# A decoder block on one Trainium2 core: additions and a gate leave GpSimd for VectorE, and weights are split 1024 elements at a time

## Chip, cores and metric

The kernel runs on one core of one Trainium2 chip. The metric is the device time of one execution in microseconds (us), and a kernel's time is the median over its runs. The engines are named as in the profile: PE (TensorE; PEld is its weight load), DVE (VectorE), ACT (ScalarE), POOL (GpSimd) and SP (SyncE, which only issues DMAs here).

## What is computed

One decoder layer on x of 256 tokens by 1024 columns, all in float32:

```
mod = silu(c) @ w_ada + b_ada                       # 1024 x 6144
shift1, scale1, gate1, shift2, scale2, gate2 = split(mod, 6)
h = rms_norm(x, g_norm_mix) * (1 + scale1) + shift1
z = h @ w_in                                        # four mixers' inputs, then 4 x 1024 merge logits
y_n = mixer_n(z), n = 0..3                          # attention, gated linear attention, retention, window attention
mixed = sum_n sigmoid(merge_logits_n) * (y_n @ w_branch[n])
x = x + gate1 * (mixed @ w_out)
h2 = rms_norm(x, g_norm_ffn) * (1 + scale2) + shift2
x = x + gate2 * moe(h2)                             # 32 experts, the top 4 of each token, clamped SwiGLU
return rms_norm(x, g_final)
```

The change touches only what comes before the experts, called the front here: the six modulation vectors, the projections by `w_in`, `w_branch` and `w_out`, and the first residual sum.

## The kernel before

**Precision.** The front's products are made from three fp32r matmuls each: an operand is split into a high part (a copy rounded to fp32r) and a low part (the rest), and high by high, low by high and high by low are added up in PSUM. `split` (L308) does it for a weight tile: ACT writes the high part (L320), DVE subtracts it from the source (L321). The two parts live in pool `wp` with `WP` = 4 buffers of 512 columns each, so splits run ahead of the matmuls by a few pieces at most. Every engine works through its own instructions in order, so an instruction that waits holds up all that is queued behind it on that engine.

**Blocks.** For each of four blocks of 256 rows of `w_in`, `h_block` (L358) makes the block's scale and shift from columns of `w_ada` by matmuls, then the normed input's high part `hh` and low part `hl` (L376, every second one on POOL). The first 1024 columns of z (four tiles `c`) are summed up over these blocks.

**Units.** The other columns of z come in units of 256 columns (`z_unit`, L337): four splits of 128x512 (two rows of K by 256 columns), each followed by twelve matmuls of 128x256 (L334). After each split one step of a mixer (`bg()`) and one step of a modulation sum (`slow_step()`) are put into the program. The mixers are generators, so their instructions stand between those of the units.

**Modulation sums.** gate1, shift2, scale2 and gate2 are summed off the matmul engine by `ada` (L209), 512 columns at a time (`s_` is the vector, `j` the half): rows k = 0..3 are scaled on ACT (L223; for gate1 on POOL, L221) and added on POOL (L225), rows 4..7 are multiplied and added on DVE (L228) into `acs`. `ada_end` (L233) sums over the partitions by four PE transposes, a DVE reduction (L241) and a small addition (L242).

**Merge.** Sixteen units follow, four for each mixer branch in the order 0, 3, 1, 2 (`bi` counts them; unit 4 * `bi` + `u`). Each does a `z_unit`, a sigmoid on ACT (`msg`, L773), two splits of 128x256 of `w_branch` (`wl_b`, L774), twelve matmuls `pu` (L781), and on DVE `pu` * `msg` (L788). The sum over the branches, `mix`, is added on POOL (L789), on DVE for the last branch. At units 1, 3, ... 11 a modulation sum is ended and the next begun. In the last branch `mix` is split, and rows of `w_out` are loaded, multiplied by gate1 on POOL in 128x512 pieces (L746), split (`wl_o`) and multiplied with `mix` into `pw` (L737). `out_last` (L825) adds `pw` to `x_sb` on DVE (L830); the second norm and the router follow.

**Loads.** All weights go through a ring of 1 MB tiles, in the program's order on SP's queue: nine slots, from the third branch on sixteen. A load waits until the tile that its slot held has been read for the last time. The experts' weights follow in the same ring. Two late small loads, `b_down` and `g_final`, are issued by POOL (L926, L929).

## Time and profile before

| | |
|---|---|
| median of 3 runs | 1285.72 us (1283.94 to 1287.75) |
| span of the profiled execution (first to last instruction) | 1282.5 us |
| PE / DVE / ACT / POOL busy in it | 1208.7 / 484.3 / 204.4 / 134.3 us |
| moved | 469.90 MB, mean 366 GB/s |
| front / experts and last norm | first 321 us / the other 961 us |

The profiled execution's own time is not listed apart from its span; the span leaves out what lies before the first and after the last instruction, and it stands 3.2 us under the median of the runs. Busy time is summed over a window; a PE matmul's busy figure includes its pipeline, so two matmuls in a row overlap, and the distance between their starts is what one costs. "Idle before" is the time for which the engine did nothing ahead of the row, with the event that ended it.

### The profile page before, as it was taken

The page shows a single profiled execution, that of the slowest core. Times are in us where ns is not written, and L with a number is a line of the kernel's source. Part 1 is how long each engine was busy: PE and PEld are TensorE (multiplying, and loading weights), DVE is VectorE, ACT ScalarE, POOL GpSimd, SP SyncE. Part 2 cuts the span into 40 slices and gives each one's busy share as a digit, 9 for nine tenths or more (in the row PEclk, how much of TensorE's full clock was granted, in tenths as well). Part 3 has the DMA queues.
Part 4 walks back from the last instruction along what each step waited for, and adds up shares of the span by engine and source line. Part 5 has one row for each costly group of instructions (what it writes and reads, how often), then busy time and mean ns, then how long its engine had stood idle before and what let it go on. Part 6 is the DMA issues. An engine that isn't in the chain of part 4 may idle for free.

```text
span 1282.5 us, 15260 instructions
## 1 busy us (share of the span) xinstructions
PE 1208.7 (94%) x6202; PEld 568.3 (44%) x6202; DVE 484.3 (38%) x829; ACT 204.4 (16%) x403; POOL 134.3 (10%) x173
## 2 busy tenths in 40 slices
...
GB/s 337 333 191 259 117 239 393 372 102 290 291 371 398 421 414 420 413 419 417 417 418 416 419 414 421 413 421 413 422 413 421 414 420 415 418 417 415 419 380 154
DMA packets 117653, 469.90 MB, mean 366 GB/s; under 512 B 9933, under 2 KB 30506, under 8 KB 84810
## 3 DMA queue, kind: packets, MB, share of 16 engines
...
q0 software_dynamic: 192, 0.66, 0.2%
q10 hardware_dynamic: 408, 0.56, 0.1%
...
HBM read 467.80 MB, written 1.05 MB: 366 GB/s over the span
## 4 chain that ended last, share of the span: by engine, by line
PE 65%; DMA 19%; DVE 11%; issue 2%; ACT 1%; POOL 1%; ACTq 0%; POOLq 0%; SPq 0%; DVEq 0%
PE ea L1036 16%; PE eb L1036 14%; DMA wg<-in_w_gate_up_dram 12%; PE ed L1062 11%; DMA wd<-in_w_down_dram 5%; PE pz_m L334 4%; PE py L1072 4%; PE pg L971 2%; PE pw L737 2%; PE eb L1029 2%; PE pdl L1096 1%; PE ea L1029 1%; PE eat L1049 1%; PE pu L781 1%; DMA win_m<-in_w_in_dram 1%
## 5 line engine op out<-in xcount | busy, mean ns | idle before, releaser
L1036 PE MATMUL ea<-wg,he 128*64 128x512 f32 x1024 | 343.1, 600 | 7.0 <-DMA wg<-in_w_gate_up_dram 7.0
L1036 PE MATMUL eb<-wg,he 128*64 128x512 f32 x1024 | 336.9, 594 | 0.0
L1062 PE MATMUL ed<-wd,aT 128*64 128x512 f32 x960 | 216.1, 599 | 9.6 <-DMA wd<-in_w_down_dram 8.5
L1036 PEld LDWEIGHTS ea<-wg,he 128*64 128x64 f32 x1024 | 88.6, 136 | 168.3 <-issue 137.5
L1012 DVE TENSOR_SCALAR eg<-ea 128x512 f32<-128x512 f32 x32 | 22.1, 691 | 370.3 <-PE ea L1036 366.3
L1036 PEld LDWEIGHTS eb<-wg,he 128*64 128x64 f32 x1024 | 96.0, 137 | 146.8 <-issue 146.2
L1014 ACT ACTIVATE es<-eg 128x512 f32<-128x512 f32 x32 | 20.1, 630 | 844.1 <-DVE eg L1012 844.1
L1062 PEld LDWEIGHTS ed<-wd,aT 128*64 128x64 f32 x960 | 66.2, 137 | 146.9 <-issue 120.1
L995 POOL TENSOR_TENSOR pc<-pm,comb 128x128 f32<-128x128 f32 x64 | 23.5, 403 | 694.0 <-PE psm L1003 634.5
L334 PE MATMUL pz_m<-hh,wl_m 128*128 128x256 f32 x256 | 73.0, 285 | 3.1 <-DVE wl_m L321 3.0
L334 PE MATMUL pz_m<-hh,wh_m 128*128 128x256 f32 x256 | 73.4, 287 | 0.0
L334 PE MATMUL pz_m<-hl,wh_m 128*128 128x256 f32 x256 | 71.9, 281 | 0.0
L321 DVE TENSOR_TENSOR wl_m<-win_m,wh_m 128x512 fp32r<-128x512 f32 x64 | 53.5, 844 | 10.9 <-ACT wh_m L320 10.7
L1074 DVE TENSOR_TENSOR x_sb<-x_sb,py 128x512 f32<-128x512 f32 x60 | 41.2, 687 | 30.7 <-PE py L1072 30.7
L334 PEld LDWEIGHTS pz_m<-hh,wl_m 128*128 128x128 f32 x256 | 48.7, 190 | 5.1 <-DVE wl_m L321 4.9
L1029 PE MATMUL eb<-bgu,ident 32*64 32x512 f32 x128 | 49.2, 612 | 0.0
L334 PEld LDWEIGHTS pz_m<-hl,wh_m 128*128 128x128 f32 x256 | 49.0, 191 | 0.1
L334 PEld LDWEIGHTS pz_m<-hh,wh_m 128*128 128x128 f32 x256 | 48.7, 190 | 0.3
L320 ACT ACTIVATE wh_m<-win_m 128x512 fp32r<-128x512 f32 x64 | 38.8, 628 | 51.7 <-PE pz_m L334 18.5
L1065 DVE TENSOR_TENSOR oa<-ed,late 64x512 f32<-64x512 f32 x15 | 10.2, 683 | 96.0 <-PE ed L1062 96.0
L1065 DVE TENSOR_TENSOR ob<-ed,late 64x512 f32<-64x512 f32 x15 | 10.2, 683 | 91.2 <-PE ed L1062 91.2
L225 POOL TENSOR_TENSOR wada<-wada 128x512 f32<-128x512 f32 x24 | 36.8, 1532 | 61.6 <-ACT wada L223 60.8
...
## 6 DMA issues: line engine op xcount, KB each, us to landing
wg<-in_w_gate_up_dram SPq DMA_DIRECT2D x256, 1024.0 KB, 19.4
wd<-in_w_down_dram SPq DMA_DIRECT2D x120, 1024.0 KB, 19.1
...
win_c<-in_w_in_dram SPq DMA_DIRECT2D x10, 1024.0 KB, 11.8
...
```

The lines of the kernel that those rows point to most:

```text
L225: G.tensor_tensor(w[0], w[0], w[k], ALU.add)
L320: A.activation(wk, sk, AF.Copy)
L321: V.tensor_tensor(lk, sk, f32(wk), ALU.subtract)
L334: T.matmul(pz[:, b * 256:(b + 1) * 256], l, r, start=(kh == 0 and b == 0 and kk == 0 and i == 0), stop=last and i == 2, skip_group_check=True)
L737: T.matmul(pw[t, hf_], m_[:, kk, t * P:(t + 1) * P], w[:, 0, :], start=(k == 0 and i == 0), stop=(k == KC - 1 and i == 2))
L971: last_i["pg"] = T.matmul(pg[:, kk * 256:(kk + 1) * 256], n2[:, t, k * P:(k + 1) * P], pm[:, t].rearrange("p e s -> p (e s)"), start=(i == 0),
L995: G.tensor_tensor(pc[:, t, :, var, i ^ var, :], pv_[:, :, i, :], cv[:, :, i].unsqueeze(2).to_broadcast([P, EB // 2, CAP]), ALU.mult)
L1029: T.matmul(pp_[64 * j:64 * j + 64, :], ident[r:r + NE, r + e:r + e + 1].to_broadcast([NE, CAP]), bgu[r:r + NE, :], start=True, stop=False, ...
L1036: T.matmul(pp_[64 * j:64 * j + 64, :], he[:, k, (e % EB) * CAP:(e % EB + 1) * CAP], w[:, i * DE + j * 512:i * DE + (j + 1) * 512], start=F ...
L1062: T.matmul(pd[64 * jj:64 * jj + 64, :], aT[:, k % 4, 64 * (k // 4):64 * (k // 4) + 64], w[k % 2][:, o * 512:(o + 1) * 512], start=(k == 0) ...
L1072: T.matmul(py, s_[:, hf_, t * P:(t + 1) * P], o, start=True, stop=True)
L1074: V.tensor_tensor(yv, yv, py, ALU.add)
```

## The change

1. `split` makes pieces of up to 1024 elements per partition: the tiles of `wp` are twice as wide, with `WP` = 3 buffers. A unit has two splits of 128x1024 in place of four of 128x512, `w_branch` one of 128x512 in place of two of 128x256, `w_out` one of 128x1024 per row tile in place of two of 128x512.
2. `ada(s_, i)` loads 512 rows by 1024 columns (`i` is now the half of the rows) and sums all eight row tiles on DVE, 128x1024 at a time: one TENSOR_SCALAR and seven SCALAR_TENSOR_TENSOR per vector. ACT and POOL have no part in it. A step of `ada` is one row tile, so a call has four steps where it had eight.
3. `hl` and the `mix` addition are always on DVE.
4. `w_out` is no longer multiplied by gate1. `out_last` multiplies `pw` by gate1 (`gx`) and then adds it to `x_sb`, both on DVE.
5. `w_branch` comes as one tile, and the two late small loads are issued by ACT.

```diff
-WP = 4
+WP = 3
...
-    def ada(s_, j):
+    def ada(s_, i):
+        w = load_rows(f"wada{s_}_{i}", w_ada[0, i * 512:(i + 1) * 512, s_ * D:(s_ + 1) * D], D)
...
-            for k in range(4):
-                if s_ == 2:
-                    G.tensor_tensor(w[k], w[k], cact[:, k:k + 1].to_broadcast([P, 512]), ALU.mult)
+            for kk in range(4):
+                k = 4 * i + kk
+                if k == 0:
+                    V.tensor_scalar(acc, w[kk], cact[:, k:k + 1], None, ALU.mult)
                 else:
-                    A.activation(w[k], w[k], AF.Copy, scale=cact[:, k:k + 1])
-                if k:
-                    G.tensor_tensor(w[0], w[0], w[k], ALU.add)
+                    V.scalar_tensor_tensor(acc, w[kk], cact[:, k:k + 1], acc, ALU.mult, ALU.add)
                 yield
-            for k in range(4, KC):
-                V.scalar_tensor_tensor(acc, w[k], cact[:, k:k + 1], w[0] if k == 4 else acc, ALU.mult, ALU.add)
-                yield
...
     def ada_end(s_, i):
...
+        if i == 0:
+            return
...
-        for kh in range(4):
-            wh, wl = split(tiles[kh // 2][:, 2 * (kh % 2):2 * (kh % 2) + 2, c0:c0 + 256], 2, 256, f"{name}_{kh}", sw)
-            z_part(pz, wh, wl, kh, token)
-            bg()
-            slow_step()
+        for i in range(2):
+            wh, wl = split(tiles[i][:, :, c0:c0 + 256], 4, 256, f"{name}_{i}", sw)
+            for j in range(2):
+                z_part(pz, wh[:, 2 * j:2 * j + 2, :], wl[:, 2 * j:2 * j + 2, :], 2 * i + j, token)
+                bg()
+                slow_step()
...
-            (G if kk else V).tensor_tensor(hl[:, k, :], hf, f32(hh[:, k, :]), ALU.subtract)
+            V.tensor_tensor(hl[:, k, :], hf, f32(hh[:, k, :]), ALU.subtract)
...
-            for w in (wo[k], wo[k + 1]):
-                for h in range(2):
-                    c = slice(h * 512, (h + 1) * 512)
-                    G.tensor_tensor(w[:, c], w[:, c], gate1[:, c], ALU.mult)
-        cs = slice(hf_ * 512, (hf_ + 1) * 512)
-        held[k, hf_] = split(wo[k][:, cs].unsqueeze(1), 1, 512, f"o{k}{hf_}")
+        if hf_ == 0:
+            wh, wl = split(wo[k].rearrange("p (h f) -> p h f", h=2), 2, 512, f"o{k}")
+            for h in range(2):
+                held[k, h] = wh[:, h:h + 1, :], wl[:, h:h + 1, :]
...
-            wsp = [split(wb[k][:, u * 256:(u + 1) * 256].unsqueeze(1), 1, 256, f"b{n}_{u}{k}") for k in range(2)]
+            wbh, wbl = split(wb[:, :, u * 256:(u + 1) * 256], 2, 256, f"b{n}_{u}")
...
-                (V if bi == 3 else G).tensor_tensor(mv, mv, sg, ALU.add)
+                V.tensor_tensor(mv, mv, sg, ALU.add)
...
-        V.tensor_tensor(x_sb[:, t, cs], x_sb[:, t, cs], pw[t, g], ALU.add)
+        tm = mp.tile([P, 512], F32, tag="t2", name=f"gx{t}{g}")
+        V.tensor_tensor(tm, pw[t, g], gate1[:, cs], ALU.mult)
+        V.tensor_tensor(x_sb[:, t, cs], x_sb[:, t, cs], tm, ALU.add)
...
-    G.dma_start(bdn, b_down[0])
+    A.dma_start(bdn, b_down[0])
...
-    G.dma_start(gfin, g_final.rearrange("(o d) -> o d", o=1).to_broadcast([P, D]))
+    A.dma_start(gfin, g_final.rearrange("(o d) -> o d", o=1).to_broadcast([P, D]))
```

The change moves instructions on POOL and DVE. The rows below are each engine's instructions in program order: line, operation, output<-inputs, size. On POOL in the merge, before, with `wada` the rows of `w_ada` (from shift2's second half on), `mix` the sum over branches and `hrsgla`, `hrsret` tiny powers of the mixers' norms (three rows of `wo`, four products each, follow):

```order
L225 TENSOR_TENSOR wada_10_1791<-wada_10_1791 128x512 x3
L225 TENSOR_TENSOR wada_00_2040<-wada_00_2040 128x512 x3
L498 TENSOR_TENSOR hrsgla<-hvargla,mhalf 128x8
L498 TENSOR_TENSOR hrsret<-hvarret,mhalf 128x8
L225 TENSOR_TENSOR wada_10_2262<-wada_10_2262 128x512 x3
L789 TENSOR_TENSOR mix<-mix,msg_0_2229 128x512
L225 TENSOR_TENSOR wada_00_2470<-wada_00_2470 128x512 x3
L789 TENSOR_TENSOR mix<-mix,msg_1_2339 128x512
L789 TENSOR_TENSOR mix<-mix,msg_2_2437 128x512
L225 TENSOR_TENSOR wada_10_2696<-wada_10_2696 128x512 x3
L789 TENSOR_TENSOR mix<-mix,msg_3_2547 128x512
L789 TENSOR_TENSOR mix<-mix,msg_0_2663 128x512
```

and now, from the first norm to the first expert, nothing being left out:

```order
L278 TENSOR_TENSOR rsa_174<-msa_172,mhalf 128x1
L492 TENSOR_TENSOR hrsgla<-hvargla,mhalf 128x8
L492 TENSOR_TENSOR hrsret<-hvarret,mhalf 128x8
L863 TENSOR_TENSOR ssq_3155<-ssq_3155,mhalf 128x1 x2
L887 TENSOR_TENSOR n2l<-scr,n2h 128x256 x2
L988 TENSOR_TENSOR pc_3595<-pm_3368,comb 128x2x64 x8
```

All of the sums and products with 512 columns have left POOL. On DVE in the merge, unit 5 before (`wl_m` low parts of `w_in`, `wl_b` of `w_branch`, `acs` the modulation sum):

```order
L321 TENSOR_TENSOR wl_m_1_0_2269<-win_m_00_2156,wh_m_1_0_2268 128x512
L321 TENSOR_TENSOR wl_m_1_1_2286<-win_m_00_2156,wh_m_1_1_2285 128x512
L788 TENSOR_TENSOR msg_0_2229<-pu_0_2239,msg_0_2229 128x512
L241 TENSOR_REDUCE ade_2259<-pmt_2254 128x4
L321 TENSOR_TENSOR wl_m_1_2_2304<-win_m_01_2158,wh_m_1_2_2303 128x512
L242 TENSOR_TENSOR modT<-ade_2259,bT 128x4
L321 TENSOR_TENSOR wl_m_1_3_2322<-win_m_01_2158,wh_m_1_3_2321 128x512
L321 TENSOR_TENSOR wl_b_10_2342<-wb_0_2154,wh_b_10_2341 128x256
L228 SCALAR_TENSOR_TENSOR acs_2266<-wada_11_2264,cact,wada_10_2262 128x512
L228 SCALAR_TENSOR_TENSOR acs_2266<-wada_11_2264,cact,acs_2266 128x512
L321 TENSOR_TENSOR wl_b_11_2346<-wb_0_2154,wh_b_11_2345 128x256
L228 SCALAR_TENSOR_TENSOR acs_2266<-wada_11_2264,cact,acs_2266 128x512
```

and now, from the end of unit 4 to the end of unit 5:

```order
L315 TENSOR_TENSOR wl_m_0_1_2009<-win_m_01_1977,wh_m_0_1_2008 128x1024
L315 TENSOR_TENSOR wl_b_0_2039<-wb_1973,wh_b_0_2038 128x512
L221 SCALAR_TENSOR_TENSOR acs_1878<-wada_1_0_2057,cact,acs_1878 128x1024
L269 COPY gate_1517<-pb_0_2338 128x512
L221 SCALAR_TENSOR_TENSOR acs_1878<-wada_1_0_2057,cact,acs_1878 128x1024
L315 TENSOR_TENSOR wl_m_1_0_2063<-win_m_00_1975,wh_m_1_0_2062 128x1024
L221 SCALAR_TENSOR_TENSOR acs_1878<-wada_1_1_2059,cact,acs_1878 128x1024
L315 TENSOR_TENSOR wl_m_1_1_2093<-win_m_01_1977,wh_m_1_1_2092 128x1024
L780 TENSOR_TENSOR msg_0_2036<-pu_0_2042,msg_0_2036 128x512
L221 SCALAR_TENSOR_TENSOR acs_1878<-wada_1_1_2059,cact,acs_1878 128x1024
L781 TENSOR_TENSOR mix<-mix,msg_0_2036 128x512
L315 TENSOR_TENSOR wl_b_1_2125<-wb_1973,wh_b_1_2124 128x512
```

The pieces are half as many and twice as long, the two `wl_b` of a unit are one, and the `mix` addition and the modulation steps of 1024 columns stand between them. At the merge's end, before, on DVE, with `pw` the sums over `w_out`, `x1T` a copy for the router:

```order
L830 TENSOR_TENSOR x_sb<-x_sb,pw_3106 128x512
L321 TENSOR_TENSOR wl_o_3570<-wo_0_3551,wh_o_3569 128x512
L830 TENSOR_TENSOR x_sb<-x_sb,pw_3107 128x512
L830 TENSOR_TENSOR x_sb<-x_sb,pw_3108 128x512
L868 TENSOR_TENSOR ssq_3543<-ssq_3543 128x1
L869 TENSOR_SCALAR ssq_3543<-ssq_3543 128x1
L830 TENSOR_TENSOR x_sb<-x_sb,pw_3109 128x512
L843 COPY x1T_3662<-pnt_3657 128x512
```

and now:

```order
L823 TENSOR_TENSOR gx_3211<-pw_2790,gate_1517 128x512
L824 TENSOR_TENSOR x_sb<-x_sb,gx_3211 128x512
L823 TENSOR_TENSOR gx_3220<-pw_2791,gate_1517 128x512
L824 TENSOR_TENSOR x_sb<-x_sb,gx_3220 128x512
L823 TENSOR_TENSOR gx_3229<-pw_2792,gate_1517 128x512
L824 TENSOR_TENSOR x_sb<-x_sb,gx_3229 128x512
L861 TENSOR_TENSOR ssq_3155<-ssq_3155 128x1
L823 TENSOR_TENSOR gx_3262<-pw_2793,gate_1517 128x512
L837 COPY x1T_3270<-pnt_3265 128x512
L824 TENSOR_TENSOR x_sb<-x_sb,gx_3262 128x512
```

A multiplication by gate1 stands ahead of each addition to `x_sb`, and the last addition stands behind a copy for the router.

## Rows read from the trace of the kernel before

**Rows 1.** The page: busy time of each engine over the span.
```profile
PE 1208.7 (94%) x6202; PEld 568.3 (44%) x6202; DVE 484.3 (38%) x829; ACT 204.4 (16%) x403; POOL 134.3 (10%) x173
```

**Rows 2.** Eight stretches: bounds, length, busy PE, PEld, DVE, ACT, POOL, PEclk, DMA share, GB/s.
```profile
0.00:56.00 56.00, 44.12 (x352) 32.22 (x353) 26.56 (x69) 21.50 (x42) 13.80 (x43) 1.00 0.98 331
56.00:97.00 41.00, 39.08 (x275) 32.58 (x274) 40.69 (x91) 23.62 (x65) 15.60 (x12) 1.00 0.66 224
97.00:142.00 45.00, 42.43 (x315) 35.78 (x315) 28.63 (x53) 26.05 (x52) 9.46 (x6) 0.89 0.67 233
142.00:183.00 41.00, 38.88 (x308) 36.35 (x308) 32.67 (x59) 21.25 (x39) 12.49 (x8) 1.00 0.43 141
183.00:255.00 72.00, 64.86 (x531) 63.20 (x530) 64.38 (x84) 34.83 (x66) 36.89 (x23) 0.98 1.01 381
255.00:297.00 42.00, 40.16 (x288) 37.21 (x288) 32.34 (x44) 20.84 (x38) 12.79 (x8) 1.00 0.44 160
297.00:321.00 24.00, 21.34 (x145) 16.79 (x143) 18.87 (x48) 11.80 (x28) 4.26 (x6) 1.00 0.73 269
321.00:1282.40 961.40, 917.81 (x3999) 314.13 (x3998) 240.20 (x387) 44.54 (x79) 29.05 (x69) 0.99 0.99 401
```

**Rows 3.** Waits of PE, 56 to 297 us: total us, times, longest us.
```profile
PE pu L781 <- DVE wl_b L321: 7.5, 6, 2.4
PE pz_m L334 <- DVE wl_m L321: 3.0, 5, 1.3
PE po_gla L640 <- DVE glat L627: 2.2, 2, 1.7
```

**Rows 4.** Timeline of PE, 229 to 239 us: start, us, instruction [idle before <-releaser].
```profile
230.85 0.28 PE L334 MATMUL pz_m<-hl,wh_m 128*128 128x256 f32 x1
230.97 0.28 PE L334 MATMUL pz_m<-hh,wl_m 128*128 128x256 f32 x1
...
234.60 0.38 PE L781 MATMUL pu<-yh,wl_b 128*128 128x256 f32 x1 [2.40 <-DVE wl_b L321]
```

**Rows 5.** Groups of POOL, 0 to 322 us: count | busy us, mean ns | idle before.
```profile
L225 POOL TENSOR_TENSOR wada<-wada 128x512 f32<-128x512 f32 x24 | 36.8, 1532 | 61.6 <-ACT wada L223 60.8
L746 POOL TENSOR_TENSOR wo<-wo,gate 128x512 f32<-128x512 f32 x16 | 26.1, 1663 | 0.0
L789 POOL TENSOR_TENSOR mix<-mix,msg 128x512 f32<-128x512 f32 x8 | 14.1, 1765 | 38.4 <-DVE msg L788 38.4
```

**Rows 6.** Groups of DVE, 0 to 322 us.
```profile
L321 DVE TENSOR_TENSOR wl_m<-win_m,wh_m 128x512 fp32r<-128x512 f32 x64 | 53.5, 844 | 10.9 <-ACT wh_m L320 10.7
L830 DVE TENSOR_TENSOR x_sb<-x_sb,pw 128x512 f32<-128x512 f32 x4 | 2.7, 687 | 2.5 <-PE pw L737 2.4
L376 DVE TENSOR_TENSOR hl<-hf,hh 128x256 fp32r<-128x256 f32 x4 | 1.7, 421 | 0.1
```

**Rows 7.** Timeline of DVE and, in one row, POOL, 204 to 239 us.
```profile
206.25 0.69 DVE L321 TENSOR_TENSOR wl_m<-win_m,wh_m 128x512 fp32r<-128x512 f32 x1 [0.66 <-ACT wh_m L320]
...
208.40 1.41 DVE L321 TENSOR_TENSOR wl_m<-win_m,wh_m 128x512 fp32r<-128x512 f32 x1
...
209.22 5.20 POOL L225 TENSOR_TENSOR wada<-wada 128x512 f32<-128x512 f32 x3
209.73 1.26 DVE L242 TENSOR_TENSOR modT<-ade,bT 128x4 f32<-128x4 f32 x1
...
231.37 1.77 DVE L228 SCALAR_TENSOR_TENSOR acs<-wada,cact,wada 128x512 f32<-128x512 f32 x1
...
236.51 0.75 DVE L228 SCALAR_TENSOR_TENSOR acs<-wada,cact,acs 128x512 f32<-128x512 f32 x1
```

**Rows 8.** Groups of ACT, 0 to 322 us.
```profile
L278 ACT ACTIVATE xn<-x_sb 128x1024 f32<-128x1024 f32 x2 | 2.1, 1048 | 2.9 <-PE pv L199 2.9
```

**Rows 9.** Two short stretches around 130 us, columns as in rows 2.
```profile
126.00:130.00 4.00, 1.79 (x15) 1.29 (x13) 4.00 (x9) 0.63 (x1) 1.40 (x1) 0.94 0.79 257
130.00:134.00 4.00, 4.00 (x15) 3.13 (x14) 0.57 (x2) 0.09 (x1) 0.00 (x0) 0.50 1.03 397
```

More of the change, by code (lines that the diff above doesn't have):

```diff
@@ L207, in hybrid_block_kernel @@
     acs = {}
-    def ada(s_, j):
-        w = []
-        for i in range(2):
-            t = wtile(f"wada{s_}_{j}{i}").rearrange("p (k f) -> p k f", f=512)
-            nc.sync.dma_start(t, w_ada[0, i * 512:(i + 1) * 512, s_ * D + j * 512:s_ * D + (j + 1) * 512].rearrange(
-                "(k p) f -> p k f", p=P))
-            w += [t[:, k, :] for k in range(4)]
-        acc = acs[s_, j] = mp.tile([P, 512], F32, tag="acs", name=f"acs{s_}{j}", bufs=1)
+    def ada(s_, i):
+        w = load_rows(f"wada{s_}_{i}", w_ada[0, i * 512:(i + 1) * 512, s_ * D:(s_ + 1) * D], D)
+        if i == 0:
+            acs[s_] = mp.tile([P, D], F32, tag="acs", name=f"acs{s_}", bufs=1)
+        acc = acs[s_]
@@ L229, in run, with ada_end @@
                 yield
         slow.append(run())
-    def ada_end(s_, j):
+    def ada_end(s_, i):
         while slow:
             slow_step()
-        acc = acs.pop((s_, j))
-        pt = bank("t", f"pmt{s_}{j}")
-        for kk in range(4):
-            T.transpose(pt[:, kk * P:(kk + 1) * P], acc[:, kk * P:(kk + 1) * P], ident)
-        col = cp.tile([P, 4], F32, tag="ade", name=f"ade{s_}{j}")
-        V.tensor_reduce(col, pt.rearrange("p (k r) -> p k r", k=4), AX.X, ALU.add)
-        V.tensor_tensor(modT[:, s_, 4 * j:4 * j + 4], col, bT[:, s_, 4 * j:4 * j + 4], ALU.add)
+        if i == 0:
+            return
+        acc = acs.pop(s_)
+        for j in range(2):
+            pt = bank("t", f"pmt{s_}{j}")
+            for kk in range(4):
+                T.transpose(pt[:, kk * P:(kk + 1) * P], acc[:, (4 * j + kk) * P:(4 * j + kk + 1) * P], ident)
+            col = cp.tile([P, 4], F32, tag="ade", name=f"ade{s_}{j}")
+            V.tensor_reduce(col, pt.rearrange("p (k r) -> p k r", k=4), AX.X, ALU.add)
+            V.tensor_tensor(modT[:, s_, 4 * j:4 * j + 4], col, bT[:, s_, 4 * j:4 * j + 4], ALU.add)
```

48 lines of the change are left out of this document (22 added, 26 removed).

## The prediction

> **What bounds the kernel now.** I read the page first: PE is busy for 1208.7 of 1282.5 us, DVE for 38%, POOL for 10% [rows 1]. Those shares are averages over two kernels in one: the table by stretches [rows 2] shows them apart. After 321 us PE is busy for 917.8 of 961.4 us and the DMA share is 0.99, and the change puts nothing there. So only the front can give, and the question is how much of its 321 us PE spends unfed.
>
> PE's busy figure hides this, because a matmul's record includes its pipeline: two 128x256 matmuls start 0.12 us apart while each counts 0.28 [rows 4]. I therefore price a stretch by its count of matmuls at 0.118 us. From 183 to 255 us, 531 x 0.118 = 62.7 of 72 us: 9.3 us unfed. From 142 to 183, 308 x 0.118 = 36.3 of 41: 4.7. From 97 to 142, 315 x 0.118 = 37.2 of 45: 7.8. From 56 to 97, 275 x 0.118 = 32.5 of 41: 8.5. For 255 to 297 the same price would give 8.0, but 48 of the matmuls there (`pw`: four rows k, two halves, two token tiles, three products) are 512 columns wide, and 48 x 0.118 = 5.7 more leaves about 2.3. In all some 33 us; this is the most that better feeding can give.
>
> What does PE wait for? The list of its waits names low parts that DVE is late with, `wl_b` 7.5 us and `wl_m` 3.0, and `glat` 2.2 [rows 3]. These waits are fewer than the unfed time, since a stop also drains the pipe.
>
> Why is DVE late? POOL's groups show 24 + 16 + 8 additions and products of 128x512, at 1.53 to 1.77 us each [rows 5]: 77 us in the front. DVE's own groups show the other side. A 128x512 subtraction costs 0.687 us where nothing disturbs it (the `x_sb` group), but `wl_m` averages 0.844 over 64 [rows 6]. The timeline shows which ones are long: at 206.25 `wl_m` takes 0.69; at 208.40, as POOL's work begins, 1.41, and an addition of **4 columns** takes 1.26 us just after 209.22, where POOL starts three additions. `acs` takes 1.77 us at 231.37 and 0.75 at 236.51 [rows 7]. A 4-column addition has no work to be slow at: DVE waits for something that POOL holds. That 1.77 us stands directly ahead of the `wl_b` for which PE then waits for 2.40 us [rows 4]. From 183 to 255 DVE is busy for 64.4 of 72 us with POOL at 36.9 beside it, from 56 to 97 for 40.7 of 41 [rows 2]. In these stretches DVE sets the pace, and part of its time is the collision.
>
> **The change, term by term.** New durations: DVE's 128x256 subtraction takes 0.421 and its 128x512 one 0.687 [rows 6], so 256 columns cost 0.266 us, 1024 columns 0.687 + 0.53 = 1.22 us, and the modulation step (0.75 at 512 [rows 7]) 1.28. ACT's 1024-column copy has a row of its own kind: 1.05 [rows 8].
>
> *183 to 255 us* (eight merge units, four pairs of 18 us). DVE before, undisturbed, per pair: 8 x 0.69 + 4 x 0.42 + 2 x 0.69 + 4 x 0.75 + one reduction and small addition 0.85 = 12.4 us; the trace has 64.4/4 = 16.1, so some 3.7 us per pair is collision. After: 4 x 1.22 + 2 x 0.69 (`wl_b`) + 2 x 0.69 (`msg`) + 2 x 0.69 (`mix`, from POOL) + 4 x 1.28 + 0.85 = 15.0. PE needs 62.7/4 = 15.7 per pair. So DVE's sum is at 95% of PE's even though it takes POOL's work over, and it is 1 us below what it is busy for now. The floor is 62.7, a gain of 9.3; with DVE this full and in order, and pieces only three deep, I leave a quarter of the unfed time: **-7** (bounds 0 and -9.3).
>
> *56 to 97 and 97 to 142* (attention, gated linear attention). POOL's 15.6 and 9.5 us go, and with them most of the excess on DVE; against it stand gate1's eight steps at 1.28 for eight at 0.75, +4.2 us of DVE over both stretches. DVE's slack before was nil in the first. I take **-5** of 8.5 (bounds 0, -8.5). In the second, PE falls to the lower level of its clock, 1.2 GHz: 0.50 granted from 130 to 134 us, right after the wait for `glat`, in which PE was busy for 1.79 of 4 us [rows 9]. The mean of the stretch is 0.89 [rows 2]: 0.11 x 45 = 5 us of work lost, so some 10 us at half speed. `glat` still stands in DVE's queue behind steps that are now longer (1.28 + 1.22), so the wait need not go, and the level may fall again; **-4** of 7.8 (bounds 0, -7.8).
>
> *142 to 183*: -3 of 4.7 (0 to -4.7). *255 to 297*: no POOL additions to `mix` before, but POOL's 12.8 us of `wo` products go, and two splits in place of four: -2 of 2.3 (0 to -2.3).
>
> *0 to 56*: loads pace it (DMA share 0.98, PE 44 of 56 us [rows 2]). `hl` on DVE costs 0.42 us where DVE is half idle: nothing, covered by the loads. The first piece is twice as long (ACT 1.05 by row against about 0.63, DVE 1.22 against 0.69), once on the path: **+0.5**; bounds -0.8 and +3, if every block pays.
>
> *297 to 321*: four multiplications by gate1 of 0.69 on DVE, each between the last `pw` and `x_sb`. DVE idled 2.4 us in all before the four additions, waiting for PE [rows 6], so two can lie in that; the last is on the path, the one before it partly: **+1.2** (bounds 0 and 4 x 0.69 = +2.8). ACT now issues two small loads; ACT is busy for 11.8 of 24 us there [rows 2], and this is costed at nothing; if its queue covers nothing, two issues cost no more than about 1 us.
>
> *After 321*: costed at nothing, if the gain arrives. The loads of the expert ring begin before 255; from 255 to 321 the DMAs idle for 0.56 x 42 + 0.27 x 24 = 30 us, waiting for tiles to come free. A front shorter by less than that just starts the experts with the ring as full as before.
>
> The sum: -5 -4 -3 -7 -2 +0.5 +1.2 = -19.3 us against the span of 1282.5, so 1263.2. The median of the runs stands 3.2 above that span, so **1266 us**.
>
> **A rule against it.** `acs` with two SBUF operands took 0.75 us where the plain two-operand subtraction took 0.687 [rows 6, 7]: 9% more. The Trainium skill, "Vector Engine (DVE) Microarchitecture Reference", section "Points that are easy to get wrong", says that this instruction with two SBUF sources that are not bf16 runs at half throughput; these rows disagree. It is a rival below because the change puts 28 such steps of 1024 columns on DVE's path.
>
> **Rivals.**
> 1. *DVE becomes the bound* (slower). Everything POOL and ACT did for the sums is now on DVE, in order. A long step (1.28), `msg` and `mix` (0.69 each) may stand ahead of a 1.22 us split: 3.9 us, plus ACT's 1.05, against some 24 matmuls x 0.118 = 2.8 us that one piece feeds, two pieces ahead at most. For: 95% load; in order; half as many, larger pieces. Against: the load falls from 16.1 to 15.0 per pair. The twelve merge units from 142 to 255 us have three pieces each. If each of the 36 made PE wait 1 us longer, +36 would meet the -19: 1303. It decides at 19 / 36 = 0.53 us per piece: below that the net is a gain. At 0.25 us each the gain halves: 1275.
> 2. *Steps at half throughput*: if twice the columns cost twice the 0.53 us per 512, a step takes 1.28 + 2 x 0.53 = 2.3 us; 4 x 1.0 us more per pair makes DVE 19.1 us against today's 18, +4 in the merge, and the rest of the gains about gone in the mixers: near 1285. The row at 236.51 speaks against it.
> 3. *The gain is absorbed*: the experts' loads run at 0.99 share [rows 2]; if the ring is not full at the end of the front, the experts wait for what the front saved: 1284 to 1287. Against: the 30 us of idle DMA. Or POOL was not the cause and PE's unfed time stays.
> 4. *All of it*: nearly all unfed time goes, half clock too: -30 us, 1255.
>
> **How the numbers follow.** Forecast with parts of its terms off by up to half (1258 to 1274): 0.62. Rival 4: 0.10. Rival 1 in its halved form (1274 to 1281): 0.08, in its slower form: 0.09. Rivals 2 and 3: 0.03 and 0.08. A difference under 0.3% (3.9 us) can't be told from none. Faster by more than that, below 1281.9: 0.62 + 0.10 + 0.08, 0.80. Within it: 0.10, from rivals 2 and 3 for the most part. Slower, above 1289.6: 0.10. The range leaves out the slower cases and the bottom of rival 4: 1252 to 1282.
>
> **What would show it.** Right: POOL empty from 56 to 297 us but for two tiny powers; `wl_m` at 1.2 us, `acs` near 1.28 with no 1.8 or 2.4 us ones, the 4-column addition at 0.16; PE's wait for `wl_b` near nothing; the first expert matmul some 19 us before 321. The clock near 1.00 from 97 to 142 would show the half level gone. Wrong: DVE full in 183 to 255 with PE waiting for `wl_m` at each piece (rival 1), `acs` above 2 us (2), PE waiting for `wg` early in the experts (3), or the same unfed time with an empty POOL.

## The result and the profile after

| | before | after |
|---|---|---|
| median of the runs beside each other | 1285.38 us (4 runs) | 1266.61 us (4 runs, 1261.97 to 1266.64) |
| ratio, 95% interval | | 0.986 (0.9833 to 0.9886) |
| span of the profiled execution | 1282.5 us | 1264.9 us |

The change gains 18.8 us, 1.5%. A second measurement of the same kernel, on another chip, gave 1267.68 against 1282.86 us, 0.9881 (0.9858 to 0.9903). The forecast was 1266. How far its terms hold is seen stretch by stretch; here each stretch is bounded by the first matmul of a unit or an expert, in both traces:

| stretch | before | after | difference | forecast |
|---|---|---|---|---|
| start to the first unit (blocks) | 56.4 | 54.7 | -1.7 | +0.5 |
| first four units (attention) | 40.4 | 37.9 | -2.5 | -5 |
| next four (gated linear attention) | 45.0 | 37.3 | -7.7 | -4 |
| merge units 0 to 3 | 41.0 | 41.1 | +0.1 | -3 |
| merge units 4 to 11 | 71.8 | 62.2 | -9.6 | -7 |
| merge units 12 to 14 | 35.1 | 31.9 | -3.2 | -2 |
| unit 15 to the gather of the first experts (`pg`) | 26.7 | 28.8 | +2.1 | +1.2 |
| gather to the second expert | 19.0 | 22.4 | +3.4 | 0 |
| second expert to the end | 947.1 | 948.6 | +1.5 | 0 |
| sum (span) | 1282.5 | 1264.9 | -17.6 | -19.3 |

The busy time of the engines over the span [rows 1]:

```profile
PE 1205.8 (95%) x6202; PEld 563.2 (45%) x6202; DVE 454.3 (36%) x763; ACT 177.5 (14%) x297; POOL 42.9 (3%) x111
```

POOL lost 91 of 134 us. DVE took work over and is busy for 30 us **less** than before. The groups of DVE in the front, with count, busy us, mean ns and idle time, show where that comes from [rows 6, 7]:

```profile
L315 DVE TENSOR_TENSOR wl_m<-win_m,wh_m 128x1024 fp32r<-128x1024 f32 x32 | 38.9, 1222 | 12.6 <-ACT wh_m L314 12.6
L221 DVE SCALAR_TENSOR_TENSOR acs<-wada,cact,acs 128x1024 f32<-128x1024 f32 x28 | 35.8, 1279 | 0.0
L315 DVE TENSOR_TENSOR wl_b<-wb,wh_b 128x512 fp32r<-128x512 f32 x16 | 11.0, 687 | 1.1 <-ACT wh_b L314 1.1
L238 DVE TENSOR_TENSOR modT<-ade,bT 128x4 f32<-128x4 f32 x8 | 1.3, 158 | 0.0
```

Every form now has its undisturbed duration: 1.22 us and 1.28 us as worked out, and the 4-column addition that took 1.26 us beside POOL takes 0.158. The page of the Trainium skill that speaks against the step (half throughput with two SBUF sources that are not bf16, "Vector Engine (DVE) Microarchitecture Reference", section "Points that are easy to get wrong") is not borne out: 1.279 us for the step, 1.222 for the plain subtraction.

The stretches of the changed kernel, columns as in [rows 2]:

```profile
54.70:92.60 37.90, 37.90 (x266) 31.44 (x264) 30.80 (x78) 22.74 (x58) 0.00 (x0) 1.00 0.77 276
92.60:129.90 37.30, 36.72 (x309) 32.08 (x308) 28.95 (x45) 19.02 (x32) 0.00 (x0) 1.00 0.74 254
129.90:171.00 41.10, 39.97 (x317) 37.06 (x317) 30.68 (x49) 15.88 (x22) 4.20 (x2) 1.00 0.53 180
171.00:233.20 62.20, 61.87 (x530) 60.79 (x529) 54.81 (x67) 25.79 (x34) 0.00 (x0) 1.00 1.03 400
233.20:265.10 31.90, 31.90 (x231) 29.98 (x231) 19.87 (x24) 14.56 (x18) 0.00 (x0) 1.00 0.49 179
265.10:296.40 31.30, 27.35 (x192) 22.46 (x190) 22.10 (x49) 13.85 (x27) 2.71 (x4) 0.98 0.51 184
```

POOL is empty but for two powers of 2.6 and 1.6 us. In merge units 4 to 11 DVE is busy for 54.8 of 62.2 us, 88%, and PE takes 0.117 us per matmul (62.2 / 530): fully fed. What PE still waits for, from 54 to 296 us [rows 3]:

```profile
PE pg L964 <- DVE pm L946: 1.7, 2, 1.4
PE pl L839 <- DVE x1T L837: 1.6, 2, 0.9
PE pz_m L328 <- DVE wl_m L315: 1.0, 2, 0.8
PE pgb L585 <- DVE glm L580: 0.6, 1, 0.6
PE pl L860 <- DVE sel L859: 0.4, 1, 0.4
...
PE pnt L831 <- DVE x_sb L824: 0.3, 1, 0.3
```

The waits for `wl_b` (7.5 us) and `glat` are gone, and those for `wl_m` are down from 3.0 to 1.0. Most of what is left (`pg`, `pl`, `pnt`: 4.0 us) stands at the end of the front, and it has a price there that its own length doesn't show. In the four-microsecond stretches of that place the granted clock falls to half:

```profile
284.00:288.00 4.00, 2.79 (x33) 1.48 (x31) 2.35 (x6) 1.48 (x4) 0.00 (x0) 1.00 0.02 4
288.00:292.00 4.00, 2.94 (x31) 2.56 (x30) 3.21 (x16) 3.60 (x10) 1.12 (x2) 1.00 0.01 2
292.00:296.00 4.00, 2.35 (x18) 2.00 (x17) 3.70 (x8) 1.04 (x3) 1.59 (x2) 0.92 0.40 113
296.00:300.00 4.00, 4.00 (x15) 1.94 (x16) 1.82 (x5) 0.56 (x1) 0.00 (x0) 0.50 0.97 312
300.00:304.00 4.00, 4.00 (x10) 0.98 (x12) 2.81 (x11) 2.10 (x3) 0.00 (x0) 0.50 1.01 421
```

PE is busy for 2.79, 2.94 and 2.35 of 4 us while the router is worked out, and then runs at 1.2 GHz for some ten microseconds into the first expert. Before, the fall was at 130 us [rows 9]. At the end of the front the kernel before had 2.5 us of waits, and the clock stayed at 1.00 there, though PE was hardly busier in the last two of these three rows:

```profile
306.00:310.00 4.00, 3.98 (x35) 2.68 (x34) 1.02 (x4) 2.31 (x6) 0.56 (x1) 1.00 0.80 266
310.00:314.00 4.00, 3.17 (x35) 2.17 (x33) 3.40 (x13) 3.09 (x8) 0.56 (x1) 1.00 0.72 268
314.00:318.00 4.00, 2.21 (x19) 1.77 (x17) 3.70 (x12) 1.74 (x5) 2.02 (x3) 1.00 0.80 326
```

The changed kernel reaches the second expert 19.1 us sooner (316.3 against 335.4), with the same 267 matmuls since unit 15. Its first expert begins 24.6 us sooner (296.4 against 321.0), but this is no measure: before, 26 matmuls of the gather stood ahead of it, and now 12 do.

### The profile page after: what moved, and what is told of

It reads as the page before. It is cut to its first block, busy times and chain, and to the rows that moved or that the text cites. A ratio compares the mean times of both kernels' runs of the same rounds, so it can differ in the third digit from the quotient of the medians.

```text
span 1264.9 us, 14895 instructions
## 1 busy us (share of the span) xinstructions
PE 1205.8 (95%) x6202; PEld 563.2 (45%) x6202; DVE 454.3 (36%) x763; ACT 177.5 (14%) x297; POOL 42.9 (3%) x111
## 3 DMA queue, kind: packets, MB, share of 16 engines
q10 hardware_dynamic: 600, 1.22, 0.3%
## 4 chain that ended last, share of the span: by engine, by line
PE 73%; DMA 18%; DVE 6%; ACT 1%; issue 1%; POOL 0%; POOLq 0%; DVEq 0%; SPq 0%; ACTq 0%
PE ea L1029 16%; PE eb L1029 14%; DMA wg<-in_w_gate_up_dram 12%; PE ed L1055 11%; PE pz_m L328 6%; DMA wd<-in_w_down_dram 5%; PE py L1065 4%; PE pg L964 2%; PE eb L1022 2%; PE pw L731 2%; PE ea L1022 1%; PE pdl L1089 1%; PE pu L773 1%; PE eat L1042 1%; PE pm L248 1%
## 5 line engine op out<-in xcount | busy, mean ns | idle before, releaser
L1029 PE MATMUL ea<-wg,he 128*64 128x512 f32 x1024 | 337.7, 602 | 6.9 <-DMA wg<-in_w_gate_up_dram 6.8
L1029 PE MATMUL eb<-wg,he 128*64 128x512 f32 x1024 | 331.4, 596 | 0.0
L1007 ACT ACTIVATE es<-eg 128x512 f32<-128x512 f32 x32 | 20.2, 630 | 845.8 <-DVE eg L1005 845.8
L1058 DVE TENSOR_TENSOR oa<-ed,late 64x512 f32<-64x512 f32 x15 | 10.2, 682 | 96.0 <-PE ed L1055 96.0
L314 ACT ACTIVATE wh_m<-win_m 128x1024 fp32r<-128x1024 f32 x32 | 34.0, 1061 | 71.3 <-PE pz_m L328 63.4
L315 DVE TENSOR_TENSOR wl_m<-win_m,wh_m 128x1024 fp32r<-128x1024 f32 x32 | 38.9, 1222 | 12.6 <-ACT wh_m L314 12.6
L1058 DVE TENSOR_TENSOR ob<-ed,late 64x512 f32<-64x512 f32 x15 | 10.2, 682 | 89.6 <-PE ed L1055 89.6
L1065 PE MATMUL py<-oa,sm 128*128 128x512 f32 x60 | 33.8, 645 | 5.1 <-DVE oa L1059 5.1
```

Of the source, the lines that this page charges most:

```text
L314: A.activation(wh, src, AF.Copy)
L315: V.tensor_tensor(wl, src, f32(wh), ALU.subtract)
L1029: T.matmul(pp_[64 * j:64 * j + 64, :], he[:, k, (e % EB) * CAP:(e % EB + 1) * CAP], w[:, i * DE + j * 512:i * DE + (j + 1) * 512], start=F ...
L1065: T.matmul(py, s_[:, hf_, t * P:(t + 1) * P], o, start=True, stop=True)
```

## The experiments

All ratios are against the kernel before on the same chip, since its median moved between 1280.4 and 1284.3 us from chip to chip.

| run | edit | median us | ratio, 95% interval |
|---|---|---|---|
| e1_off_pool | the sums off POOL, pieces of 512 | 1264.72 | 0.9863 (0.9837 to 0.9889) |
| e2_wide_alone | pieces of 1024, POOL as before | 1276.92 | 0.9948 (0.9932 to 0.9965) |
| e3_idle_pool | after + 24 POOL additions on a private tile | 1281.56 | 0.9975 (0.9959 to 0.9991) |
| e6_copy_pool | after + 24 POOL copies | 1269.80 | 0.9894 (0.9858 to 0.9929) |
| e7_mix_pool | after, `mix` additions on POOL | 1266.14 | 0.9891 (0.9866 to 0.9915) |
| e4_gate_wo | after, gate1 into `w_out` on DVE | 1260.83 | 0.9822 (0.9805 to 0.9838) |
| e10_gate_wo_again | the same | 1260.56 | 0.9834 (0.9809 to 0.9859) |
| e8_gate_wo_512 | the same with pieces of 512 | 1263.45 | 0.9861 (0.9835 to 0.9886) |
| e9_after_again | after | 1267.68 | 0.9881 (0.9858 to 0.9903) |
| e5_fill | after + 17 matmul calls in the last waits | 1262.84 | 0.9859 (0.9834 to 0.9884) |
| e11_fill_banks | the same, other banks | 1264.84 | 0.9866 (0.9843 to 0.9889) |
| e12_no_gate_sum | after without gate1's sum | 1267.32 (one run) | |

Lengths of the stretches in us, bounds as in the table above:

| stretch | before | after | e1 | e2 | e3 | e6 | e7 | e8 | e10 | e11 |
|---|---|---|---|---|---|---|---|---|---|---|
| first four units | 40.4 | 37.9 | 37.7 | 38.7 | 38.1 | 38.1 | 38.1 | 37.7 | 37.9 | 38.1 |
| next four | 45.0 | 37.3 | 37.3 | 41.5 | 38.2 | 37.4 | 37.3 | 37.3 | 37.4 | 37.4 |
| merge 0 to 3 | 41.0 | 41.1 | 42.6 | 43.5 | 46.0 | 42.4 | 41.2 | 42.7 | 41.2 | 41.1 |
| merge 4 to 11 | 71.8 | 62.2 | 62.3 | 69.0 | 72.4 | 64.8 | 63.4 | 62.9 | 62.1 | 62.6 |
| unit 15 to the second expert | 45.7 | 51.2 | 50.5 | 45.7 | 46.9 | 51.2 | 49.4 | 44.9 | 45.1 | 47.8 |

In the last row e1 can't be compared with the others: 16 more matmuls of the first expert stand ahead of the second one there. The changed kernel's 51.2 us came out in its second profile (e9) as well.

### Is it POOL, or the number of DVE instructions?

Two things were changed at once, so each was made alone. Both runs also have what was not tried apart: the two small loads on ACT, and a setting of the program, `dynamic_dma_scratch_size=1024`, which is part of the changed kernel. e1 relieves ACT as well, of the 24 products that it made for the sums; the next run tells POOL's part from ACT's.

```diff
 # e1: before, with ada, hl, mix and gate1 as after; split() and WP = 4 as before
-                (V if bi == 3 else G).tensor_tensor(mv, mv, sg, ALU.add)
+                V.tensor_tensor(mv, mv, sg, ALU.add)
...
 # e2: after, with ada, hl, mix and gate1 as before; split() and WP = 3 as after
-                V.tensor_tensor(mv, mv, sg, ALU.add)
+                (V if bi == 3 else G).tensor_tensor(mv, mv, sg, ALU.add)
```

> All of the change except the wide pieces: splits stay at 512 columns with four buffers, two splits of 256 for w_branch; the sums, mix, hl and gate1 leave POOL. Collision theory (POOL's 128x512 operations hold DVE up): most of the gain is here, 1264 to 1272 us; wl_m back at 0.69 us, acs at 1.28. By the sum of DVE's durations a pair of merge units takes 8 x 0.69 + 4 x 0.42 + 4 x 0.69 + 4 x 1.28 + 0.85 = 15.9 us against PE's 15.7, so some waits may stay. Rival (fewer and larger DVE instructions bring the gain): 1276 to 1284 us.

> The wide pieces alone: 1024-column splits with three buffers, but the sums on ACT and POOL, mix, hl and the product of w_out with gate1 on POOL as before. Collision theory: wl_m well over 1.22 us on average, the waits for wl_b stay, 1280 to 1288 us. Rival (fewer instructions bring the gain): 1267 to 1274 us.

Taking the work off POOL alone gives 0.9863, the whole of the change. (To some 3 us: its clock fell at the end of the front for a shorter time, 0.57 granted from 292 to 296 us and 1.00 in the rows on either side.) Its DVE groups are undisturbed although there are more instructions than in the kernel before (845 against 829):

```profile
L317 DVE TENSOR_TENSOR wl_m<-win_m,wh_m 128x512 fp32r<-128x512 f32 x64 | 43.3, 688 | 9.5 <-ACT wh_m L316 9.5
L317 DVE TENSOR_TENSOR wl_b<-wb,wh_b 128x256 fp32r<-128x256 f32 x32 | 12.9, 422 | 5.9 <-ACT wh_b L316 5.9
```

The wide pieces alone give 0.9948, 7.4 us, somewhat more than the collision theory had allowed (1276.9, expected 1280 to 1288) and less than the rival. Its rows fit: `wl_m` is long, but there are half as many instructions to be caught.

```profile
L319 DVE TENSOR_TENSOR wl_m<-win_m,wh_m 128x1024 fp32r<-128x1024 f32 x32 | 44.0, 1375 | 15.1 <-ACT wh_m L318 15.1
L319 DVE TENSOR_TENSOR wl_b<-wb,wh_b 128x512 fp32r<-128x512 f32 x16 | 14.2, 885 | 2.3 <-ACT wh_b L318 2.3
```

The kernel before has `wl_m` at 53.5 us [rows 6] and this for `wl_b`:

```profile
L321 DVE TENSOR_TENSOR wl_b<-wb,wh_b 128x256 fp32r<-128x256 f32 x32 | 22.3, 709 | 3.5 <-ACT wh_b L320 3.5
```

Against the 43.3 and 12.9 us of e1 its two groups are 10.2 + 9.4 us too long; those of e2, against 38.9 and 11.0 in the changed kernel, only 5.1 + 3.2. So the pieces are for the most part a second way to the same gain, not an addition: once POOL is empty, they are worth 1.5 us (merge 0 to 3: 42.6 in e1, 41.1 after; 4 to 11: 62.3 and 62.2).

### POOL work whose result nobody reads

The sharpest test adds POOL work and changes no other engine's instructions. `spare` is read by nobody; what still hangs on POOL is the buffer of the high part that it reads, which ACT may fill again only afterwards.

```diff
             wh, wl = split(tiles[i][:, :, c0:c0 + 256], 4, 256, f"{name}_{i}", sw)
+            if name in idle_units:      # merge units 0 to 11
+                G.tensor_tensor(spare, spare, f32(wh[:, 0:2, :]).rearrange("p k f -> p (k f)"), ALU.add)
```

> The changed kernel with 24 added POOL additions of 128x512 in the first twelve merge units, two per unit, on a tile that nothing else reads; each reads the high part of a piece. They are about as much POOL work as stood there before (37 us from 183 to 255). Collision theory: wl_m and acs lengthen from 1.22 and 1.28 to 1.6 or more on average in the merge though no instruction of DVE waits for POOL, PE waits for low parts again, and the time rises by 6 to 14 us: 1273 to 1281. Rival (the load of POOL does not matter to DVE, only what is queued on DVE): 1265 to 1268 us.

The time went back to 1281.6 us, just above the range for a collision and far above the rival's 1265 to 1268. (The ten runs lie between 1277.2 and 1284.0; the trace is of the first, 1277.2.) The groups of DVE and, in the last row, of POOL:

```profile
L315 DVE TENSOR_TENSOR wl_m<-win_m,wh_m 128x1024 fp32r<-128x1024 f32 x32 | 44.1, 1384 | 12.8 <-ACT wh_m L314 12.8
L221 DVE SCALAR_TENSOR_TENSOR acs<-wada,cact,acs 128x1024 f32<-128x1024 f32 x28 | 40.3, 1438 | 0.0
L786 DVE TENSOR_TENSOR mix<-mix,msg 128x512 f32<-128x512 f32 x12 | 9.3, 774 | 0.0
L785 DVE TENSOR_TENSOR msg<-pu,msg 128x512 f32<-128x512 f32 x12 | 8.2, 682 | 0.0
...
L336 POOL TENSOR_TENSOR spare<-spare,wh_m 128x512 f32<-128x512 f32 x24 | 43.6, 1818 | 178.2 <-ACT wh_m L314 178.2
```

`wl_m`, `acs` and `mix` are longer than in the changed kernel (1.22, 1.28, 0.687 us); `msg`, which has one operand in PSUM, is not: 682 ns here and 685 there. The means stay under the 1.6 us that were expected, since only the instructions that meet an addition are caught. One such meeting in the timeline, two additions on POOL and four rows of DVE:

```profile
158.29 2.95 POOL L336 TENSOR_TENSOR spare<-spare,wh_m 128x512 f32<-128x512 f32 x2
...
158.36 1.77 DVE L499 TENSOR_TENSOR hynret<-hocret,hrsret 128x512 f32<-128x512 f32 x1 [1.17 <-POOL hrsret L497]
160.05 1.74 DVE L515 TENSOR_TENSOR gsggla<-gsggla,z_gr 128x512 f32<-128x512 f32 x1
161.71 1.21 DVE L315 TENSOR_TENSOR wl_m<-win_m,wh_m 128x1024 fp32r<-128x1024 f32 x1
...
165.70 0.68 DVE L515 TENSOR_TENSOR gsgret<-gsgret,z_rg 128x512 f32<-128x512 f32 x1
```

The same product of 128x512 takes 1.74 us beside POOL and 0.68 without. The 4-column addition is long again, too, beside an addition whose sum nobody reads:

```profile
209.25 1.29 POOL L336 TENSOR_TENSOR spare<-spare,wh_m 128x512 f32<-128x512 f32 x1 [3.07 <-ACT wh_m L314]
209.28 1.28 DVE L238 TENSOR_TENSOR modT<-ade,bT 128x4 f32<-128x4 f32 x1
```

And it goes both ways. The durations of the 24 additions (min / median / max in ns), and from the timeline a subtraction that began 0.11 us ahead of one of them:

```profile
L336 POOL TENSOR_TENSOR spare<-spare,wh_m x24: 1276/1802/2678, 120.9 to 239.8; 128x512 f32<-128x512 f32 x24
```

```profile
237.01 1.23 DVE L315 TENSOR_TENSOR wl_m<-win_m,wh_m 128x1024 fp32r<-128x1024 f32 x1 [0.64 <-ACT wh_m L314]
...
237.12 2.27 POOL L336 TENSOR_TENSOR spare<-spare,wh_m 128x512 f32<-128x512 f32 x1 [5.10 <-ACT wh_m L314]
```

Here DVE began first and took its normal 1.23 us, and the addition, 1.28 alone, took 2.27: the later one waited for about as long as the earlier one ran. In these rows they don't share, they take turns by whole instructions. The Trainium skill says so too, in "SBUF — State Buffer", section "SBUF: two separate sides": the pair of ports that VectorE and GpSimd share is locked for a whole instruction by the one that starts first, for VectorE among others when both of its inputs are in SBUF and GpSimd's instruction reads SBUF. These rows agree with it, that of `msg` included.

Not all of the 15 us that the merge lost (46.0 + 72.4 against 41.1 + 62.2) is collision: POOL's additions stood ahead of `hrsgla` and `hrsret`, which the mixers wait for, and ACT waited once for 4.0 us for `hrsgla` and once for 1.9 us for an addition. The waits for the powers stand in merge 0 to 3. The four DVE groups with the largest excess (the three above and `wl_b`) are 11.8 us longer. In merge 4 to 11 DVE is busy for 66.2 us in place of 54.8, with 68 instructions in place of 66, and PE waits seven times, 7.7 us in all, where the changed kernel has one wait of 0.2; each time for a low part ahead of which DVE had no idle time. There it is DVE that is late, and not ACT.

The same with copies, which have one input:

```diff
-                G.tensor_tensor(spare, spare, f32(wh[:, 0:2, :]).rearrange("p k f -> p (k f)"), ALU.add)
+                G.tensor_copy(spare, f32(wh[:, 0:2, :]).rearrange("p k f -> p (k f)"))
```

> The run with POOL work on a private tile once more, with copies of 128x512 (one input) in place of the 24 additions (two inputs). If any POOL work holds DVE up in proportion to its time: the DVE forms lengthen about as with the additions per us of POOL, 1272 to 1282 us. If it takes POOL's two inputs from SBUF: wl_m at 1.22 us, acs at 1.28, and 1264 to 1268 us.

Neither expectation fits whole. The groups of DVE and POOL:

```profile
L315 DVE TENSOR_TENSOR wl_m<-win_m,wh_m 128x1024 fp32r<-128x1024 f32 x32 | 40.6, 1275 | 11.5 <-ACT wh_m L314 11.5
L221 DVE SCALAR_TENSOR_TENSOR acs<-wada,cact,acs 128x1024 f32<-128x1024 f32 x28 | 37.3, 1331 | 0.0
...
L336 POOL COPY spare<-wh_m 128x512 f32<-128x512 f32 x24 | 28.0, 1166 | 180.3 <-ACT wh_m L314 180.3
```

DVE is held up, so two inputs on POOL are not what it takes; but the same four groups are only 4.3 us longer for 28 us of POOL, 0.15 per us, where the additions cost 11.8 for 43.6, 0.27 per us. (POOL's time includes its own waiting for DVE.) A copy takes 0.61 us at the least, an addition 1.28; a shorter hold should catch fewer instructions and keep each for less, which fits but was not tried apart. In time the run can't be told from the changed kernel (0.9894, with intervals that overlap); its trace has 3.9 us more in the merge.

Then one part of the real work alone was put back:

```diff
-                V.tensor_tensor(mv, mv, sg, ALU.add)
+                (V if bi == 3 else G).tensor_tensor(mv, mv, sg, ALU.add)
```

> The changed kernel with only the mix addition of the second and third branch back on POOL: eight additions of 128x512, about 14 us of POOL, as before. Collision theory: DVE loses eight additions of 0.69 us (5.5 us) and gets back 8 x 0.7 to 1.4 us of lengthening, so the balance on DVE is about nil or worse, 1265 to 1270 us. Rival (DVE is the bound in these units and any work taken from it pays): 1260 to 1264 us.

0.9891 (0.9866 to 0.9915): no difference that can be told from the changed kernel. Eight additions on POOL took 15.1 us, `wl_b` rose from 0.687 to 0.891 us, and merge 4 to 11 from 62.2 to 63.4. In that stretch DVE has seven instructions of 0.69 us less and is busy for as long as in the changed kernel, 54.6 us against 54.8: what was saved is given back in full, as expected.

### The end of the front, and the clock

gate1 on the path cost 2.1 us up to `pg`. What if it goes back to the rows of `w_out`, on DVE, where the last merge units leave it idle?

```diff
         if hf_ == 0:
+            V.tensor_tensor(wo[k], wo[k], gate1, ALU.mult)
             wh, wl = split(wo[k].rearrange("p (h f) -> p h f", h=2), 2, 512, f"o{k}")
...
-        tm = mp.tile([P, 512], F32, tag="t2", name=f"gx{t}{g}")
-        V.tensor_tensor(tm, pw[t, g], gate1[:, cs], ALU.mult)
-        V.tensor_tensor(x_sb[:, t, cs], x_sb[:, t, cs], tm, ALU.add)
+        V.tensor_tensor(x_sb[:, t, cs], x_sb[:, t, cs], pw[t, g], ALU.add)
```

> The changed kernel with gate1 multiplied into the rows of w_out again, but on DVE, 128x1024 at a time, ahead of the split; out_last is one addition. Theory (the four multiplications stand on the path at the end of the front, 2 us there, and the stop for them lets PE's clock fall to half from 296 to 306 us, 5 us more): 1258 to 1263 us, with the clock at 1.00 at the first expert. Rival (8 x 1.22 us more on DVE in the last merge units make the output projection wait): 1266 to 1271 us.

> The changed kernel as it is, to stand beside the next two on one chip: ratio to the kernel before 0.983 to 0.989, half clock for some 10 us at the start of the experts.

> gate1 multiplied into the rows of w_out on DVE, as in the earlier run, beside the changed kernel on the same chip. If the shorter end of the front and the clock are worth what the trace said (24.1 against 19.1 us at the second expert): 4 to 6 us under the changed kernel. If that run was merely a quicker one: within 2 us of it.

Both runs with gate1 in `w_out` (e4, e10) are at 1261 us, 7.1 us under the changed kernel beside the second one. The eight products of 1.22 us cost PE nothing (merge 12 to 14: 31.9 us with them and without). Unit 15 to the second expert takes 45.8 and 45.1 us, about as in the kernel before (45.7). The waits at the end of the front of e10, and the stretches in which the changed kernel ran at half clock:

```profile
PE pg L963 <- DVE pm L945: 1.1, 2, 0.9
PE pl L838 <- DVE x1T L836: 0.5, 1, 0.5
PE pnt L830 <- DVE x_sb L823: 0.3, 1, 0.3
```

```profile
292.00:296.00 4.00, 2.95 (x17) 1.86 (x17) 3.96 (x10) 0.00 (x0) 1.22 (x2) 1.00 0.66 196
296.00:300.00 4.00, 4.00 (x21) 1.68 (x22) 3.00 (x10) 2.67 (x4) 0.00 (x0) 1.00 0.98 368
300.00:304.00 4.00, 4.00 (x22) 1.38 (x20) 0.53 (x3) 0.00 (x0) 0.00 (x0) 1.00 1.01 425
```

1.9 us of waits in place of 4.0, and no fall. But two things changed at once, the work and the stops. To try the stops alone, the work was left as it is and PE was given something to do in them:

```diff
+    def fill(bk, n, after):
+        with tc.issue_after(after):
+            for _ in range(n):
+                T.matmul(bk[:, 256:256 + P], ident, ident, start=True, stop=True, skip_group_check=True)
...
+        if g == 1:
+            fill(pw[t, 0], 4, tr_i.ins)
...
+    fill(pp, 9, pp_i)
```

> The changed kernel with 17 added matmuls of 128x128 that write an unused part of a PSUM bank, placed where PE waits at the end of the front: four behind each of the last two groups of x1T transposes, nine behind ppos. Theory (the stops at 286 to 294 us let the clock fall to half from 296 to 306 us, which costs 5 us): the clock stays at 1.00 there, 1260 to 1263 us. Rival (the fall has nothing to do with these stops): half clock as before, 1266 to 1268 us, the added matmuls costing up to 1 us.

> The changed kernel with 17 added matmuls in PE's waits at the end of the front once more, now in banks whose content has been read, so that the router gets the same sums. If the stops let the clock fall: 1.00 in the rows from 288 to 308 us, and 2 to 5 us under the changed kernel. If the fall does not hang on the stops: half clock as before, 0 to 1 us above it.

The 17 calls are 34 matmul instructions in the trace. In e5 all three groups of added matmuls wrote to the bank in which the router's sums of the first 128 tokens are added up; that changed the sums, and the experts got other tokens. Only its front is read: the clock was 1.00 throughout, and the second expert began at 313.9 us. In e11 they write to banks that have been read. Three stretches of e11:

```profile
292.00:296.00 4.00, 3.73 (x34) 3.44 (x33) 1.63 (x10) 2.03 (x6) 1.41 (x2) 1.00 0.25 71
296.00:300.00 4.00, 3.97 (x16) 1.64 (x17) 3.21 (x9) 0.00 (x0) 0.00 (x0) 1.00 0.85 310
300.00:304.00 4.00, 4.00 (x26) 2.15 (x26) 2.65 (x7) 2.67 (x4) 0.00 (x0) 1.00 1.01 424
```

The same work with 34 matmul instructions **more** reaches the second expert at 47.8 us after unit 15, 3.4 sooner than the changed kernel's 51.2. So it is the stops that let the clock fall, and the fall costs 3.4 us or more. The multiplications by gate1 are not the only way to such stops: e2, which has none of them there, shows a short fall in the same place (0.70 and 0.88 granted over the two rows from 304 to 312 us). In time e11 is 2.8 us under the changed kernel beside it, with intervals that overlap (0.9843 to 0.9889 and 0.9858 to 0.9903): the trace shows the gain, the times of the runs alone would not. A stretch at half clock in the experts near 355 us is left in all of these kernels.

The best version with pieces of 512:

> All sums off POOL, gate1 multiplied into the rows of w_out on DVE, but pieces of 512 columns with four buffers as in the kernel before. If the wide pieces bring something of their own once POOL is empty: 1263 to 1267 us, against 1260.8 of the same kernel with wide pieces. If they bring nothing: 1259 to 1262 us.

0.9861 against 0.9822 and 0.9834 with wide pieces; the interval (0.9835 to 0.9886) overlaps with the second one's, so this too is read from the trace. It puts 1.5 us into merge 0 to 3 and 0.8 into merge 4 to 11 (42.7 and 62.9 against 41.2 and 62.1); the wide pieces are worth about two microseconds of their own here.

### Does DVE set the pace in the attention stretch?

The forecast had -5 us there and the trace -2.5. If DVE still held PE up, it must show when its load is taken away.

```diff
-                else:
+                elif s_ != 2:
                     V.scalar_tensor_tensor(acc, w[kk], cact[:, k:k + 1], acc, ALU.mult, ALU.add)
```

> The changed kernel without seven of gate1's eight summing steps (7 x 1.28 us of DVE between 55 and 130 us), so gate1 is not the reference's and the experts get other tokens; only the front's stretches are read. If DVE's load sets the pace from 55 to 93 us: that stretch takes 35 us or less where the changed kernel takes 37.9. If PE and the chain of the attention steps set it: 37 to 38 us.

The stretch in this run:

```profile
55.80:93.70 37.90, 37.90 (x266) 31.41 (x264) 27.24 (x78) 22.73 (x57) 0.00 (x0) 1.00 0.90 329
```

37.9 us, as in the changed kernel, with DVE 3.6 us lighter and PE's record full in both. PE sets the pace there, and a lighter DVE can bring no more than the -2.5 us.

## Why the prediction was right, and where it was not

The total is right to a microsecond, and its ground is shown: POOL's instructions hold up DVE's, DVE's low parts come late, PE waits. e1 gives the whole gain with the sums moved and the pieces as before, e3 takes it back with POOL work whose result nobody reads, and the forms of DVE have exactly the durations that were worked out (1.22, 1.28). But the sum came out by errors that cancel: five of the seven terms missed by 2 us or more, and the 1263.2 us of the sum stand 1.7 under the 1264.9 measured, made up for by 3.2 us added for the median, where an execution of the changed kernel takes 1.7 more than its span. That the total is right to a microsecond is luck.

- *Merge 4 to 11, -7: came out at -9.6.* The floor was right (62.7 us; 62.2 measured); leaving a quarter of the unfed time was too cautious. DVE at 88%, in order, with three buffers, makes PE wait for 0.2 us in all there. The 95% of the forecast was the sum of whole records (60 us; they overlap by 0.08 us each) with 16 steps of `acs`, of which 12 fall here. Some 1.7 us of the gain is clock, which the forecast didn't count: in the kernel before it fell there, too (0.92 and 0.66 granted over the two rows from 232 to 240 us).
- *Attention, -5, and merge 0 to 3, -3: came out at -2.5 and +0.1.* The step that failed is to "price a stretch by its count of matmuls at 0.118 us". That is the distance of two 128x256 matmuls; the stretches of the mixers hold other matmuls, transposes and narrow products, and the "unfed" 8.5 and 4.7 us were largely their real cost: the attention stretch still takes 6.5 us more than 266 x 0.118 where PE never waits for DVE. The prediction explained the gap between 33 us unfed and 12.7 us of listed waits [rows 3] by the pipe that a stop drains; the price was the larger part. The busy column said it: PE was busy for 39.1 of 41 us there [rows 2], and 37.9 of 37.9 after. In merge 0 to 3 PE is busy for 40.0 of 41.1 us; which chain of the mixers fills the rest was not tried.
- *Gated linear attention, -4: came out at -7.7.* The forecast let the half clock come back, since `glat` stands behind longer steps. The wait for `glat` went altogether and with it the fall; it is there in e2, where POOL still collides (PE waits 1.7 us for `glat`; 41.5 us), and in no run with POOL empty.
- *Merge 12 to 14, -2: came out at -3.2.* That is beyond the bound of -2.3, though the forecast's stretch reached 7 us into unit 15. e1 has the same 31.9 us with pieces of 512, e2 33.2 with POOL's products of `w_out`.
- *Blocks, +0.5: came out at -1.7.* 1.2 us of it lie ahead of the first matmul of z, whose start varied from 18.4 to 20.2 us over the profiles of the experiments, so they can't be put down to the change; the longer first piece is not seen.
- *The end of the front, +1.2: came out at +2.1 up to `pg`.* The bounds held (0 to 2.8). But behind it stands the term that was missed: "After 321: costed at nothing". The prediction looked for the half clock where it had been and not at the new stops. It cost 3.4 us up to the second expert. The other 1.5 goes with a longer stretch at half clock near 355 us (PEclk 0.50 to 0.67 over 12 us, where the kernel before had 0.74 to 0.84 over 8 us at 380), but that is no trait of the changed kernel: its second profile (e9) has 0.57 over 4 us there and takes 947.6 us behind the second expert, 0.5 more than before.
- *Rivals.* DVE did not become the bound: 88% in merge 4 to 11, with PE at 0.117 us per matmul. The experts' loads took nothing back: PE's waits for `wg` and `wd` are 6.8 and 7.9 us, before 7.0 and 8.5. The half throughput of the steps is out (1.279 us), and "all of it", -30 us, rested on the same 33 us of unfed time.
